# Experts' weights in pieces of 1 MB, the embedding's projection beside the router, and three input projections split

## The chip, the cores and the metric

The kernel runs on one core of a Trainium2 chip. The metric is the device time of one execution in microseconds. TensorE (PE) multiplies, VectorE (DVE), ScalarE (ACT) and GpSimd (POOL) work on SBUF and PSUM, and SyncE (SP) issues most of the DMAs.

## What is computed

256 tokens of width 1024, all in fp32, go through two blocks. The first has a mixer of a state-space part and attention, then a mixture of experts, then an embedding that is gated in. The second has RWKV7 beside a convolution, and then a feed-forward part. The end of the first block, where most of the change lies:

```python
h = rms_norm(x, moe_norm_w)
x = x + hier_moe(h, ...)   # 4 groups of 8 experts, width 256; best 2 of the best group
gate = jax.nn.sigmoid(rms_norm(x, ple_norm_w) @ w_ple_gate)
x = x + gate * (p @ w_ple)                # p: 256 x 256, an input of its own
```

In the second block three matrices of 1024 x 1024 (w_rkv) give r, k and v; small low-rank products give the decays and the rates; from these the scan of RWKV7 is computed.

## The kernel before

**A product.** Weights come as pieces of 128 x 1024 (0.5 MB) into the pool `raw` (four buffers). In the split way ACT makes the upper part `whi` (L238), DVE the rest `wlo` (L239), and PE multiplies whi by xh, whi by xl and wlo by xh (L275 for results with features on the partitions, L293 with tokens there). A unit of 512 output features has 32 products of 256 columns, so 96 rows of L275. In the plain way (tokens with an f in `PROG`) PE takes raw and fp32 input as they are (L266); each product is two rows of the trace, so 64 rows a unit, and ACT and DVE have no split to make.

**The order.** `PROG1` and `PROG` list units and steps. A scheduler then merges them, so that the instructions of an engine are interleaved, and every engine works through its own list in order. SP's list of DMAs is one too: one that waits for a free buffer holds those behind it. The second half's tokens are K0, K1, K2 (first half of r, k, v), R0, R1, R2 (their second half), L (low-rank products), A0 (`wkv_prep`: from k, r and L the factors AR and BK, on ACT, DVE and POOL), and B0 (L1269: products of AR and BK; G, L1271; then a DMA and the scan).

**The experts.** All 32 are computed: 8 steps q with 4 experts of 32 slots each, 24 pieces a step, 192 in all (100.7 MB). The first 38 pieces (`NFIRST`) are loaded ahead, during the mixer, into a ring of 40 buffers that are made of pools otherwise used for the mixer. P12 and P6 in `PROG1` and `expert_early` say where they are issued. Once the router has chosen (L805, L809 to L830 on DVE, L858), Pm is built, L966 gathers the tokens, L997 multiplies gate and up, L1018 down, and L1026 adds into four accumulators in PSUM (acc). They start as the residual: L949 multiplies X1 by the identity. After q = 0's gate and up all engines take a branch (L871 to L877): the `overflow` path serves experts with more than 32 tokens. In the profile it isn't taken.

**The embedding.** `ple` follows: L1034 copies acc to X, L376 transposes, L386 and L387 make xh and xl, and `ple_proj` computes U = p @ w_ple in the split way (L1056, 24 rows) before the gate's products (L293, 96 rows).

Of the kernel before, what the change touches and what calls it, by code (L numbers as in the profile page):

```python
# [100 lines left out]
def pack(i):  # L101
# [18 lines left out]
    d["w_gu"] = np.ascontiguousarray(wgu.reshape(8, 2, 2, 8, 128, 512).transpose(0, 3, 1, 4, 2, 5))  # L120
    d["w_dn"] = np.ascontiguousarray(i["w_exp_down"][0].reshape(8, 2, 2, 2, 128, 2, 512).transpose(0, 3, 5, 1, 4, 2, 6))
# [46 lines left out]
class Net:  # L168
# [535 lines left out]
    def mix1(self):  # L704
# [32 lines left out]
        self.expert_early(4)  # L737
        for c in range(2):
            self.transpose_chunk(M, c, mh, ml)
        self.expert_early(2)  # L740
        X1 = self.cst.tile([128, 2, 1024], F32, name="X1", tag="xp")
        self.ss1 = self.c1.tile([128, 2, 2], F32, name="ss1")
        self.hT = [self.mw.tile([128, 4, 256], F32, name=f"hT{c}", tag="mw") for c in range(2)]
# [54 lines left out]
    def route(self, hT, r):  # L798
# [68 lines left out]
    def overflow(self, acc, comb, rank, cnti):  # L867
# [4 lines left out]
        with tc.If(cv > 32):  # L872
# [6 lines left out]
            hT = self.hT  # L879
            gu, pt = [self.bank(tag="B") for _ in range(2)], self.bank((128, 256), "B")  # L880
            with tc.For_i(0, 8) as q:
                for e in range(4):
                    for kt in range(8):
                        w = self.t2(s="wf")
                        nc.gpsimd.dma_start(w, a["w_gu"][bass.ds(q, 1), kt, e // 2, :, e % 2, :].rearrange("o p n -> (o p) n"))
                        for tt in range(2):
                            PE.matmul(gu[tt], hT[kt // 4][:, kt % 4, tt * 128:tt * 128 + 128], w, start=(kt == 0), stop=(kt == 7))
                    wd = [[self.t2(s="wf") for _ in range(2)] for _ in range(2)]
                    for kt in range(2):
                        for h in range(2):  # L890
                            nc.gpsimd.dma_start(wd[kt][h], a["w_dn"][bass.ds(q, 1), kt, h, e // 2, :, e % 2, :].rearrange(
# [17 lines left out]
    def expert_fetch(self):  # L909

        a, n = self.a, self.wi
        q, k = divmod(n, 24)
        src = a["w_gu"][q, k // 2, k % 2] if k < 16 else a["w_dn"][q, (k - 16) // 4, (k - 16) // 2 % 2, k % 2]
        pool, tag = self.ring[n % len(self.ring)]
        if tag != "a8":
            w = pool().tile([128, 2, 512], F32, name=self.name("we"), tag=tag)
        elif self.half is None:
            self.half = self.a8(shape=(128, 4, 512), s="we")
            w = self.half[:, 0:2]
        else:  # L920
            w, self.half = self.half[:, 2:4], None
        self.nc.sync.dma_start(w, src)
        self.wi += 1
        self.early.append(w)
# [10 lines left out]
    def moe(self):  # L935
# [3 lines left out]
        self.expert_early(NFIRST - self.wi)  # L939
# [5 lines left out]

        acc = [[self.bank(tag="A", s="acc") for _ in range(2)] for _ in range(2)]
        for h in range(2):
            for tt in range(2):
                PE.matmul(acc[tt][h], self.ident, X1[:, tt, 512 * h:512 * h + 512], start=True, stop=False,  # L949
                          skip_group_check=True)  # L950
# [37 lines left out]
        nxt = gather(0)  # L988
        for q in range(8):
# [4 lines left out]
            for kt in range(8):  # L994
                w = [self.expert_piece() for i in range(2)]
                for e in range(4):
                    PE.matmul(gu[32 * e:32 * e + 32, :], xg[:, kt, 32 * e:32 * e + 32], w[e // 2][:, e % 2, :],  # L997
                              start=(kt == 0), stop=(kt == 7), skip_group_check=True)
            if q == 0:
                self.overflow(acc, comb, rank, cnti)  # L1000
# [13 lines left out]
            for kt in range(2):  # L1014
                for h in range(2):
                    w = [self.expert_piece() for i in range(2)]
                    for e in range(4):
                        PE.matmul(py[h][32 * e:32 * e + 32, :], gT[:, kt * 128 + 32 * e:kt * 128 + 32 * e + 32],  # L1018
                                  w[e // 2][:, e % 2, :], start=(kt == 0), stop=(kt == 1), skip_group_check=True)
            for h in range(2):  # L1020
# [8 lines left out]
        self.p = self.t2((128, 2, 256), s="p")  # L1029
        nc.sync.dma_start(self.p, a["pT"])  # L1030
# [9 lines left out]
    def ple_proj(self):  # L1040
# [3 lines left out]
        self.U = U = self.a8(shape=(128, 2, 1024), s="U")  # L1044
        ph, pl = (self.t2((128, 2, 256), F32R, s="ps") for _ in range(2))
        S.activation(ph, self.p, AF.Copy)
        V.tensor_sub(pl, self.p, ph.bitcast(F32))
        for c in range(2):
            hi, lo = self.split(self.fetch(a["w_ple"][c]))
            for tt in range(2):  # L1050
                ts = slice(128 * tt, 128 * tt + 128)
                ps = self.bank(tag="B")
                n = 0
                for kt in range(2):
                    for x, ww in ((ph, hi), (pl, hi), (ph, lo)):
# [689 lines left out]
```

## Time and profile before

| | us |
|---|---|
| three runs | 1242.92, 1243.56, 1244.0; median 1243.56 |
| the profiled execution | 1243.91 |
| its span, first to last instruction | 1242.2 |
| outside the span | 1.7 |
| PE busy in the span | 1146.0 (92%) |
| DVE, ACT, POOL busy | 693.8, 461.4, 109.7 |
| experts' gate, up and down, from L997's first to L1018's last row | 360.1 to 567.6 |
| mean granted clock of PE | 0.976 of full speed |

The times that are compared are those of the runs. The profile shows one execution. Its rows give starts from the span's beginning; a busy time can overlap with the next row, since matmuls are pipelined, so the distance of starts is the better measure of a group of equal rows.

### The profile page before, as it was taken

The numbers are of one execution on the slowest core, as the hardware profiler recorded it, in microseconds if no ns is written. First come the engines' busy times: TensorE is split into PE (matmuls) and PEld (weight loads), VectorE is DVE, ScalarE is ACT, GpSimd is POOL, SyncE is SP. The second block draws the span as 40 slices with busy tenths as digits, with TensorE's granted clock in tenths as the row PEclk, the third lists the DMA queues.
The fourth block names the chain that finished last, engine by engine and source line by source line (L and its number), as shares of the span: only waits on it lengthen the run. The fifth ranks groups of instructions, "written<-read, shape, count | busy, mean of one in ns | idle before, by whom it ended". The sixth has DMA issues, their size and how long they took to land.

```text
span 1242.2 us, 19656 instructions
## 1 busy us (share of the span) xinstructions
PE 1146.0 (92%) x7795; PEld 873.9 (70%) x7795; DVE 693.8 (56%) x1459; ACT 461.4 (37%) x835; POOL 109.7 (9%) x126
## 2 busy tenths in 40 slices
PE   5999999999979988877799899999999999999996
PEld 5898986667745433314697686778777788999995
DVE  4777677556532211104766527884988526656555
ACT  4644644444312000004654314332332215545453
POOL 0002321001100000000020402301200100000000
PEclk9999999999989999998899898899999999999999
DMA  8743555336769999994455244124422335555553
GB/s 301 279 157 115 153 170 180 109 118 245 276 255 409 409 409 409 409 409 168 134 182 204 93 139 125 52 70 111 111 70 69 102 125 191 177 187 186 190 186 116
DMA packets 82976, 242.20 MB, mean 195 GB/s; under 512 B 24160, under 2 KB 24416, under 8 KB 82496
## 3 DMA queue, kind: packets, MB, share of 16 engines
q1 hardware_dynamic: 80224, 231.11, 52.7%
q0 software_dynamic: 2224, 8.90, 2.5%
q8 instruction: 63, 1.03, 0.3%
q10 hardware_dynamic: 432, 0.89, 0.2%
q14 instruction: 33, 0.27, 0.1%
HBM read 234.31 MB, written 4.46 MB: 192 GB/s over the span
## 4 chain that ended last, share of the span: by engine, by line
PE 51%; DMA 8%; DVE 6%; ACT 2%; issue 1%; POOL 1%; DVEq 0%; ACTq 0%; SPq 0%; POOLq 0%
PE ps L266 12%; PE ps L275 9%; PE acc L293 7%; DMA we<-in_w_gu 5%; PE ps L1613 4%; PE ps L293 3%; PE ps L997 3%; DMA we<-in_w_dn 2%; PE ps L966 2%; PE ps L1018 2%; PE ps L1315 1%; DVE cv L1465 1%; PE acc L1026 1%; ACT whi L238 1%; PE ps L1056 1%
## 5 line engine op out<-in xcount | busy, mean ns | idle before, releaser
L239 DVE TENSOR_TENSOR wlo<-raw,whi 128x1024 fp32r<-128x1024 f32 (+1 forms) x178 | 225.7, 1272 | 149.9 <-ACT whi L238 144.8
L238 ACT ACTIVATE whi<-raw 128x1024 fp32r<-128x1024 f32 (+1 forms) x178 | 187.6, 1055 | 221.3 <-PE ps L275 78.6
L266 PE MATMUL ps<-x,raw 128*128 128x256 f32 x704 | 179.8, 402 | 5.3 <-issue 5.3
L266 PEld LDWEIGHTS ps<-x,raw 128*128 128x128 f32 x704 | 132.3, 196 | 30.9 <-issue 10.6
L275 PE MATMUL ps<-xh,whi 128*128 128x256 f32 x408 | 116.7, 287 | 4.4 <-ACT cv L446 1.5
L275 PE MATMUL ps<-xl,whi 128*128 128x256 f32 x408 | 115.1, 283 | 0.0
L275 PE MATMUL ps<-xh,wlo 128*128 128x256 f32 x408 | 114.2, 285 | 0.9 <-DVE wlo L239 0.8
L1465 DVE SCALAR_TENSOR_TENSOR cv<-up,par,cv 128x256 f32<-128x256 f32 x232 | 107.6, 500 | 2.6
L275 PEld LDWEIGHTS ps<-xh,whi 128*128 128x128 f32 x408 | 78.0, 191 | 6.8 <-ACT whi L238 3.4
L997 PE MATMUL ps<-we,xg 128*32 128x512 f32 x512 | 76.2, 597 | 4.3 <-DMA we<-in_w_gu 4.3
L275 PEld LDWEIGHTS ps<-xh,wlo 128*128 128x128 f32 x408 | 77.1, 191 | 2.1 <-DVE wlo L239 1.7
L275 PEld LDWEIGHTS ps<-xl,whi 128*128 128x128 f32 x408 | 78.1, 191 | 0.0
L275 PE MATMUL ps<-h,whi 128*128 128x256 f32 x256 | 72.1, 282 | 0.3 <-DVE l L387 0.3
L275 PE MATMUL ps<-h,wlo 128*128 128x256 f32 x256 | 71.7, 282 | 0.1
L275 PE MATMUL ps<-l,whi 128*128 128x256 f32 x256 | 71.7, 281 | 0.0
L293 PE MATMUL ps<-wlo,xh 128*128 128x512 f32 x128 | 50.7, 398 | 1.7 <-DVE wlo L239 1.7
L293 PE MATMUL ps<-whi,xh 128*128 128x512 f32 x128 | 50.9, 398 | 0.0
L293 PE MATMUL ps<-whi,xl 128*128 128x512 f32 x128 | 50.5, 394 | 0.0
L293 PE MATMUL acc<-wlo,fh 128*128 128x512 f32 x128 | 49.9, 390 | 0.0
L293 PE MATMUL acc<-whi,fl 128*128 128x512 f32 x128 | 49.9, 390 | 0.0
L293 PE MATMUL acc<-whi,fh 128*128 128x512 f32 x128 | 49.8, 389 | 0.0
L1018 PE MATMUL ps<-we,gT 128*32 128x512 f32 x256 | 44.1, 600 | 6.2 <-DVE gT L1012 3.5
(473 smaller groups left out, 2010.1 us busy)
## 6 DMA issues: line engine op xcount, KB each, us to landing
we<-in_w_gu SPq DMA_DIRECT2D x128, 512.0 KB, 10.2
we<-in_w_dn SPq DMA_DIRECT2D x64, 512.0 KB, 10.2
raw<-in_w_ff SPq DMA_DIRECT2D x64, 512.0 KB, 3.3
raw<-in_w_g SPq DMA_DIRECT2D x32, 512.0 KB, 3.3
raw<-in_w_qkv SPq DMA_DIRECT2D x24, 512.0 KB, 3.3
raw<-in_w_rkv SPq DMA_DIRECT2D x24, 512.0 KB, 3.3
raw<-in_w_o SPq DMA_DIRECT2D x16, 512.0 KB, 4.8
raw<-in_w_glu SPq DMA_DIRECT2D x16, 512.0 KB, 3.3
```

The costliest lines, as they stand in the source:

```text
L238: nc.scalar.activation(hi, r, AF.Copy)
L239: nc.vector.tensor_sub(lo, r, hi.bitcast(F32))
L266: pin(nc.tensor.matmul(out[f], r[:, k, f * 128:f * 128 + 128], xh[:, kt, :], start=(kt == 0), stop=(kt == 7)))
L275: pin(nc.tensor.matmul(out[f], w[:, k, c], x[:, kt, :], start=(kt == 0 and j == 0), stop=(kt == 7 and j == 2)))
L293: pin(nc.tensor.matmul(out[tt], x[:, x0 + k, s], w[:, k, :], start=(kt == 0 and j == 0), stop=(kt == last and j == 2)))
L966: PE.matmul(ps[:, f, :], X1[:, tt, ft * 128:ft * 128 + 128], Pm[:, tt, :], start=(tt == 0), stop=(tt == 1))
L997: PE.matmul(gu[32 * e:32 * e + 32, :], xg[:, kt, 32 * e:32 * e + 32], w[e // 2][:, e % 2, :], start=(kt == 0), stop=(kt == 7), skip_group_ ...
L1018: PE.matmul(py[h][32 * e:32 * e + 32, :], gT[:, kt * 128 + 32 * e:kt * 128 + 32 * e + 32], w[e // 2][:, e % 2, :], start=(kt == 0), stop=( ...
L1026: PE.matmul(acc[tt][h], PT[:, tt * 128:tt * 128 + 128], y, start=False, stop=(q == 7 and n == 1), skip_group_check=True)
L1056: PE.matmul(ps, x[:, kt, ts], ww[:, kt, :], start=(n == 0), stop=(n == 5))
L1465: pin(nc.vector.scalar_tensor_tensor(last, x[:, j:j + 256], self.P("cw", 8 * j + ft), o, op0=ALU.mult, op1=ALU.add))
L1613: pin(nc.tensor.matmul(out[f], r[:, k, 128 * f:128 * f + 128], z[:, kt, :], start=(kt == 0), stop=(kt == 7)))
```

## The change

Five things are edited at once.

1. Experts' pieces have 1 MB and 8 KB a partition: one piece holds a k tile of all four experts. There are 12 a step and 96 in all. The ring has 19 places; 14 take a piece as one DMA with 8 KB rows, and 5 are pairs of older buffers and take it as two DMAs with 4 KB rows. `NFIRST` is 19, the same 19.9 MB; the last of them is issued behind the first gather. `hT` is one tile, whose place is given up after the router, and `overflow` transposes X1 again.
2. p and w_ple are loaded at the end of the mixer (`ple_load`) into two of the buffers `raw`, and `ple_proj` stands right behind the router's products, in the plain way (now L1059), with U in a pool of its own. Loads and splits of it after the experts are gone.
3. The four products that start acc (L949, now L1004) come later: one before the first gather, three after q = 0's gate and up, ahead of the branch.
4. The down products go through h outside and kt inside, and y and its products for one h follow its two pieces.
5. In `PROG` K0, K2, L, K1 becomes K2, K1, K0, L, and R0, R1, R2 go from the plain way to the split way. Three pairs of later tokens change places. (`W0f` and `W1f` name the path that W0 and W1 took before; the new branch under W isn't used.)

```diff
-        q, k = divmod(n, 24)
-        src = a["w_gu"][q, k // 2, k % 2] if k < 16 else a["w_dn"][q, (k - 16) // 4, (k - 16) // 2 % 2, k % 2]
...
+        q, k = divmod(n, 12)
+        src = a["w_gu"][q, k] if k < 8 else a["w_dn"][q, (k - 8) // 2, k % 2]
+        pool, tags = self.ring[n % len(self.ring)]
+        shape = (128, 4 // len(tags), 512)
+        ws = [self.a8(shape=shape, s="we") if t == "a8" else pool().tile(list(shape), F32, name=self.name("we"), tag=t)
+              for t in tags]
+        for i, w in enumerate(ws):
+            self.nc.sync.dma_start(w, src[:, i * shape[1]:(i + 1) * shape[1], :])
...
+    def ple_load(self):
+
+        nc, a = self.nc, self.a
+        self.pp = self.act.tile([128, 1024], F32, name="pp", tag="P", bufs=2)[:, 0:512].rearrange("p (k t) -> p k t", k=2)
+        nc.sync.dma_start(self.pp, a["pT"])
+        self.wp = [self.fetch(a["w_ple"][c]) for c in range(2)]
...
+        self.ple_proj(0)
+        self.ple_proj(1)
         L = self.c1.tile([128, 2, 36], F32, name="L")
...
         nxt = gather(0)
+        self.expert_early(1)
...
             if q == 0:
+
+                for h in range(2):
+                    for tt in range(2):
+                        PE.matmul(acc[tt][h], self.ident, X1[:, tt, 512 * h:512 * h + 512], start=True, stop=False,
+                                  skip_group_check=True)
                 self.overflow(acc, comb, rank, cnti)
...
-            for kt in range(2):
-                for h in range(2):
-                    w = [self.expert_piece() for i in range(2)]
+            for h in range(2):
+                for kt in range(2):
+                    w = self.expert_piece()
...
-            hi, lo = self.split(self.fetch(a["w_ple"][c]))
...
-                for kt in range(2):
-                    for x, ww in ((ph, hi), (pl, hi), (ph, lo)):
-                        PE.matmul(ps, x[:, kt, ts], ww[:, kt, :], start=(n == 0), stop=(n == 5))
+            for kt in range(2):
+                PE.matmul(ps, self.pp[:, kt, ts], self.wp[c][:, kt, :], start=(kt == 0), stop=(kt == 1))
+            S.activation(U[:, tt, 512 * c:512 * c + 512], ps, AF.Copy)
...
-PROG = "K0 K2 L K1 A0 R0f R1f R2f B0 A1 U0f M0 C0 M0 M0 C1 G1f M0 M0 B1 O0 C2 U1f M1 C3! G0f M1 C6 M1 G3f M1 M1 C4! G2f C5 C7! O1 W0 S W1 D0 D1"
+PROG = "K2 K1 K0 L A0 R0 R1 R2 B0 A1 U0f M0 C0 M0 M0 C1 G1f M0 M0 B1 C2 O0 U1f M1 C3! C6 M1 G0f M1 G3f M1 M1 G2f C4! C5 C7! O1 W0f S W1f D0 D1"
-NEARLY = 12
-NFIRST = 38
+NEARLY = 5
+NFIRST = 19
...
-            n.ring = [(mw, "mw")] * NEARLY + [(None, "a8")] * 16 + [(raw, "raw")] * 4
-            n.ring += [(wsp, "whi"), (wsp, "wlo")] * 3 + [(mw, "mw")] * 2
+            n.ring = [(mw, ("mw",))] * NEARLY + [(None, ("a8",))] * 8 + [(wsp, ("whi", "wlo"))] * 3
+            n.ring += [(mw, ("mw",))] + [(raw, ("raw", "raw"))] * 2
```

**PE behind the router.** Before, PE's list had these rows between the router's last products (hT) and the first gather (X, Pm):

```order
L949 MATMUL acc_3318<-X_2984,const_82 128x512
L805 MATMUL ps_3227<-wr,hT_2987 128x36 [waits DVE_49]
L805 MATMUL ps_3227<-wr,hT_2986 128x36 x4
L805 MATMUL ps_3227<-wr,hT_2987 128x36 x4
L949 MATMUL acc_3320<-X_2984,const_82 128x512
L858 LDWEIGHTS ltb [waits DVE_49]
L858 MATMUL ps_3303<-sel,ltb 128x32 [waits PE_49]
```

In the changed kernel the same place reads:

```order
L806 MATMUL ps_3212<-wr,hT 128x36 x8
L1059 MATMUL ps_3233<-raw_3171,pp 128x512
L1059 MATMUL ps_3237<-raw_3173,pp 128x512 [waits DMAHW7_49,PE_49]
L1059 MATMUL ps_3237<-raw_3173,pp 128x512
L1059 MATMUL ps_3241<-raw_3173,pp 128x512 [waits Activation_49]
L1059 MATMUL ps_3241<-raw_3173,pp 128x512
L861 LDWEIGHTS ltb
L861 MATMUL ps_3304<-sel,ltb 128x32 [waits DVE_49]
```

The last product for acc has gone, and five of U's eight products (raw, pp) stand between the router and L861, which was L858; the other three have taken the places of L949 among the router's products.

**PE at the experts' end.** The last sums into acc (acc<-y), the transposes of X, and the embedding's products (ps are the split p) in the kernel before:

```order
L1026 MATMUL acc_3318<-y_4769,PT_4659 128x512 [waits DVE_49]
L1026 MATMUL acc_3320<-y_4769,PT_4659 128x512
L376 MATMUL ps_4822<-const_82,X_2984 128x128
L376 MATMUL ps_4831<-const_82,X_2984 128x128 [waits DVE_49]
L376 MATMUL ps_4840<-const_82,X_2984 128x128 [waits PE_49]
L376 MATMUL ps_4831<-const_82,X_2984 128x128 [waits DVE_49]
L376 MATMUL ps_4831<-const_82,X_2984 128x128 x2
L376 MATMUL ps_4840<-const_82,X_2984 128x128 x3
L1056 MATMUL ps_4875<-whi_4871,ps_4865 128x512 [waits DVE_49,PE_49,Activation_49]
L1056 MATMUL ps_4875<-whi_4871,ps_4866 128x512 [waits DVE_49]
```

In the changed kernel the last piece's down products (we_4813) and what follows:

```order
L1024 MATMUL ps_4782<-we_4813,gT_4779 32x512 [waits DMAHW5_49]
L1024 MATMUL ps_4782<-we_4813,gT_4779 32x512 x3
L1031 MATMUL acc_3319<-y_4819,PT_4716 128x512 [waits Activation_49]
L1031 MATMUL acc_3321<-y_4819,PT_4716 128x512
L1031 MATMUL acc_3319<-y_4820,PT_4716 128x512 [waits DVE_49]
L1031 MATMUL acc_3321<-y_4820,PT_4716 128x512
L293 MATMUL ps_4917<-whi_4921,xh_4860 128x512 [waits Activation_49]
L293 MATMUL ps_4918<-whi_4921,xh_4860 128x512
```

L1056's 24 rows are gone from here, and the gate's first products (L293) stand directly behind the last sums, ahead of half of the transposes.

**PE at R0.** Where B0's first products (AR, BK) stood before, between R0's last and R1's first products:

```order
L266 MATMUL ps_5903<-x_4807,raw_5934 128x256 x2
L1269 MATMUL ps_6061<-AR_5761,BK_5762 128x128 [waits Activation_49,Pool_49]
L1269 MATMUL ps_6062<-AR_5761,BK_5762 128x128 [waits DVE_49,Activation_49,Pool_49]
L1269 MATMUL ps_6061<-AR_5761,BK_5762 128x128 [waits Pool_49]
L266 MATMUL ps_5954<-x_4807,raw_5958 128x256 [waits DMAHW5_49,DVE_49,Activation_49]
L266 MATMUL ps_5954<-x_4807,raw_5958 128x256
```

In the changed kernel B0's products for two of four column groups stand ahead of the last 16 rows of R0:

```order
L275 MATMUL ps_5903<-xl_4855,whi_5997 128x256
L275 MATMUL ps_5904<-xh_4854,whi_5997 128x256
L275 MATMUL ps_5904<-xl_4855,whi_5997 128x256
L1270 MATMUL ps_6302<-AR_5762,BK_5763 128x128 [waits Pool_49]
L1270 MATMUL ps_6303<-AR_5762,BK_5763 128x128 [waits DVE_49,Pool_49]
L1270 MATMUL ps_6314<-AR_5762,BK_5763 128x128
L1270 MATMUL ps_6315<-AR_5762,BK_5763 128x128
```

Four more such rows of B0 follow, and only then R0's last 16. So those rows of R0, and R1 and R2 behind them, now wait for the second half of A0, which POOL finishes. Before, only three rows of B0 stood ahead of R1, and 29 came behind R2; now 14 come behind R2.

## Rows read from the trace of the kernel before

**Rows 1.** The page: traffic of the DMA engines in 40 slices of the span.
```profile
GB/s 301 279 157 115 153 170 180 109 118 245 276 255 409 409 409 409 409 409 168 134 182 204 93 139 125 52 70 111 111 70 69 102 125 191 177 187 186 190 186 116
```

**Rows 2.** Windows: busy time by engine (instructions), granted clock, DMA share, GB/s.
```profile
350.00:360.00 10.00, 6.43 (x37) 6.32 (x37) 5.97 (x35) 0.42 (x2) 0.00 (x0) 0.66 0.17 68
...
370.00:560.00 190.00, 165.56 (x1032) 66.99 (x1032) 32.30 (x88) 17.80 (x32) 0.84 (x2) 0.98 1.03 409
650.00:652.00 2.00, 1.96 (x17) 1.94 (x16) 1.22 (x5) 0.67 (x1) 0.00 (x0) 1.00 0.41 130
654.00:658.00 4.00, 3.54 (x27) 3.14 (x27) 2.30 (x6) 2.12 (x2) 0.00 (x0) 1.00 0.71 228
1000.00:1020.00 20.00, 20.00 (x94) 17.51 (x93) 5.39 (x14) 2.72 (x5) 0.00 (x0) 1.00 0.41 138
```

**Rows 3.** PE's timeline around the choice of experts: start, us, [idle before <-releaser].
```profile
348.15 1.10 PE L949 MATMUL acc<-X,const 128*128 128x512 f32 x2
352.84 0.21 PE L858 MATMUL ps<-sel,ltb 128*128 128x32 bf16 x1 [3.58 <-DVE sel L830]
...
353.89 6.26 PE L966 MATMUL ps<-Pm,X 128*128 128x128 f32 x32 [0.73 <-DVE Pm L957]
360.08 7.07 PE L997 MATMUL ps<-we,xg 128*32 128x512 f32 x64
371.31 1.04 PE L976 MATMUL ps<-comb,Pm 128*128 128x33 f32 x4 [4.15 <-PEq L872]
...
379.14 3.21 PE L1018 MATMUL ps<-we,gT 128*32 128x512 f32 x28 [0.90 <-DVE gT L1012]
```

**Rows 4.** The chain of waits around the experts' end: start, us, what.
```profile
566.60 1.01 PE ps L1018 x4
567.63 0.61 ACT y L1022
...
569.62 0.70 DVE X L1034
...
575.83 8.14 PE ps L1056 x24
583.97 21.34 PE ps L293 x94
```

**Rows 5.** The same chain in the second half's inputs.
```profile
657.55 13.69 PE ps L275 x112
...
682.85 0.72 PE ps L1246 x4
...
701.18 30.85 PE ps L266 x128
...
733.05 1.21 DVE G L1271 x2
...
735.49 1.16 PE ps L1269 x14
736.65 19.19 PE ps L266 x88
```

**Rows 6.** POOL's timeline at the end of A0.
```profile
701.56 0.73 POOL L1208 TENSOR_TENSOR BK<-rkv,cu 64x256 f32<-64x256 f32 x1
```

**Rows 7.** SP's queue from 345 to 362 us.
```profile
361.18 0.81 SPq L922 DMA_DIRECT2D we<-in_w_gu  x2
```

**Rows 8.** SP's queue of DMAs from 318 to 330 us.
```profile
318.32 4.02 SPq L230 DMA_DIRECT2D raw<-in_w_o  x3
```

**Rows 9.** SP's queue from 548 to 575 us.
```profile
547.81 6.73 SPq L922 DMA_DIRECT2D we<-in_w_dn  x6
...
562.31 0.33 SPq L230 DMA_DIRECT2D raw<-in_w_pg  x1
```

**Rows 10.** DMAs issued from 552 to 556 us: count, size, us to landing.
```profile
we<-in_w_dn SPq DMA_DIRECT2D x2, 512.0 KB, 10.2
```

**Rows 11.** The page's groups: count, busy us, mean ns, idle before.
```profile
L239 DVE TENSOR_TENSOR wlo<-raw,whi 128x1024 fp32r<-128x1024 f32 (+1 forms) x178 | 225.7, 1272 | 149.9 <-ACT whi L238 144.8
```

More of the change, by code (lines that the diff above doesn't have):

```diff
@@ L736, in mix1 @@
         mh, ml = self.a8(F32R, s="mh"), self.a8(F32R, s="ml")
[L737 removed]
+        self.expert_early(2)
         for c in range(2):
             self.transpose_chunk(M, c, mh, ml)
[L740 removed]
+        self.expert_early(1)
         X1 = self.cst.tile([128, 2, 1024], F32, name="X1", tag="xp")
         self.ss1 = self.c1.tile([128, 2, 2], F32, name="ss1")
[L743 removed]
+        self.hT = self.mw.tile([128, 2, 4, 256], F32, name="hT", tag="mw")
         self.wr = self.c1.tile([128, 8, 36], F32, name="wr")
@@ L878, in overflow @@
             V.memset(wo[1], 0.0)
-            hT = self.hT
-            gu, pt = [self.bank(tag="B") for _ in range(2)], self.bank((128, 256), "B")
+            X1 = self.X1
+            gu, pt = [self.bank(tag="B") for _ in range(2)], self.bank(tag="B")
+            pt, ht = pt[:, 0:256], pt[:, 256:512]
             with tc.For_i(0, 8) as q:
@@ L911, in expert_fetch @@
         a, n = self.a, self.wi
-        q, k = divmod(n, 24)
-        src = a["w_gu"][q, k // 2, k % 2] if k < 16 else a["w_dn"][q, (k - 16) // 4, (k - 16) // 2 % 2, k % 2]
[L914 to L922, printed above, removed]
+        q, k = divmod(n, 12)
[6 more added lines that the diff above has]
+            self.nc.sync.dma_start(w, src[:, i * shape[1]:(i + 1) * shape[1], :])
         self.wi += 1
-        self.early.append(w)
+        self.early.append([ws[e // shape[1]][:, e % shape[1], :] for e in range(4)])
     def expert_early(self, *n):
@@ L1013, in moe @@
             py = [self.bank(tag="B") for _ in range(2)]
-            for kt in range(2):
-                for h in range(2):
-                    w = [self.expert_piece() for i in range(2)]
+            for h in range(2):
+                for kt in range(2):
+                    w = self.expert_piece()
                     for e in range(4):
-                        PE.matmul(py[h][32 * e:32 * e + 32, :], gT[:, kt * 128 + 32 * e:kt * 128 + 32 * e + 32],
-                                  w[e // 2][:, e % 2, :], start=(kt == 0), stop=(kt == 1), skip_group_check=True)
-            for h in range(2):
+                        PE.matmul(py[h][32 * e:32 * e + 32, :], gT[:, kt * 128 + 32 * e:kt * 128 + 32 * e + 32], w[e],
+                                  start=(kt == 0), stop=(kt == 1), skip_group_check=True)
                 yh, yl = (self.t2(dt=F32R, s="y") for _ in range(2))
@@ L1557, in branches @@
             elif op == "W":
-                self.gated(gates[n], y, a["w_rwp"][n], pin)
+                if "f" in tok:
+                    self.gated(gates[n], y, a["w_rwp"][n], pin)
+                else:
+                    if not ys:
+                        ys = [self.keep.tile([128, 8, 256], F32R, name="y" + m, tag=f"x{m}2") for m in "hl"]
+                        self.split_act(y, *ys, V)
+                    for f, ps in enumerate(self.feat(*ys, a["w_rwp"][n], pin=pin)):
+                        V.tensor_mul(gates[n][:, f, :], ps, gates[n][:, f, :])
             elif op == "D":
```

59 lines of the change are left out of this document (27 added, 32 removed).

## The prediction

> **What bounds the kernel now.** I read the page's slices of traffic first: six slices in a row stand at 409 GB/s, which no other slice reaches [rows 1]. The windows show the same place: from 370 to 560 us the DMA engines' share is 1.03 (all 16 busy) at 409 GB/s, while PE has 165.56 us of work in 190 [rows 2]. So the experts' stage is bound by their weights, and it lasts from the first load after the ring was full to the last landing. Outside of it PE is the bound, except where it waits for a chain on other engines. Three such places are touched: the choice of experts, the embedding, and A0. The timeline of PE shows the first: 3.58 us of idle time ahead of L858, then a gather of 6.2 us in a window with a clock of 0.66 [rows 2, 3]. The chain of waits shows the second: from the last down products (566.60) it passes y, the copies of X and a split to L1056, and reaches L293 at 583.97 [rows 4]. It shows the third too: K1 ends at 671.24, R1 starts at 701.18 [rows 5], and POOL writes the last factor BK until 702.29 [rows 6].
>
> **First load after the router.** SP issues nothing for the ring until 361.18 [rows 7], because L997, which frees the first place, starts at 360.08 [rows 3]. Five of U's products now follow the router. L949 shows the price of a product of this form: two rows in 1.10 us [rows 3]; five of them overlap and take some 4.7, 5.5 at the most. So they fill 348.2 to 352.9, and L861 could not start before 352.8 anyway: they cost next to nothing there, and cover the idle time. One of the acc products falls into the 0.73 us ahead of L966. PE then enters the gather without the gap. The distance from L966 to L997 is 6.19 us at 0.66; at full clock it is 6.19 x 0.66 = 4.1. The first load comes 2.1 us earlier (bounds 0, if the clock stays low, and 3).
>
> Three acc products (2.8 us) now stand ahead of the branch, which costs PE 4.15 us in any case [rows 3]. So L1018 comes at 379.14 - 2.1 + 2.8 = 379.8. By then 16 half pieces, freed by q = 0's gate and up, have been loaded: 8.39 MB at 409 GB/s is 20.5 us from 359.1, so until about 380 and a latency. A place freed at 380.6 gives traffic again some 2 us later. I take a hole of 1.5 us (bounds 0 and 3). Both together: -0.6 us (bounds -3 and +3).
>
> L1059 also needs p and w_ple. They follow the last three loads of w_o, which SP has issued by 322.34 [rows 8], and are wanted 20 us later, so I take no wait.
>
> **Rows of 8 KB.** After the ring was full 100.66 - 19.92 = 80.74 MB are left, 197.4 us at 409 GB/s. No saturated stretch of before has longer rows. What doubling a row gives is bounded by the traffic per share: 130 / 0.41 = 317 GB/s where the low-rank weights with 2 KB rows are loaded, 228 / 0.71 = 321 and 138 / 0.41 = 337 with 4 KB rows [rows 2]. That is 1.3 to 6.3% for 2 to 4 KB. If each packet has a fixed part, the next doubling gives half as much, and 14 of 19 pieces have it: 0.5 to 2.4%, 0.9 to 4.6 us. Below, nothing: six slices at the same 409 may be a ceiling that no row length moves. I take -3 us, the middle of the two rows' results, with 0 and -4.6 as bounds.
> [...]
>
> **The embedding.** The last half piece is issued at 554.21 (six issues from 547.81, 6.73 us, less 0.33 for the last) [rows 9] and lands 10.2 us later [rows 10], at 564.4. Its products start only at 566.60, since sums of h = 0 and transposes stand ahead of them. With h outside these are done before the last piece, whose products can start as it lands. It has eight rows rather than four, so 0.8 us more at about 0.2 a row (28 rows from 379.14, 3.21 us, bound it by 0.11 [rows 3]). They end at 566.2 instead of 567.6: -1.4 us.
>
> Before, 16.4 us lie between 567.6 and L293 at 583.97: y, sums, X, then xh, the split of p and w_ple, and L1056 with 8.14 us [rows 4]. What remains is y (0.6) and its rest on DVE (as long), one split of w_pg that stands in between there (1.3 [rows 11]), two copies of X (1.4) and two parts of xl, each shorter than a copy: 5.5 us, so -10.9. w_pg was issued at 562.31 [rows 9], behind w_ple; now its buffers are freed by the pieces before the last. The steps just named are the least; if the splits of w_pg come late, 8.5.
> One thing is given back. L1056's 24 rows take 8.14 us, against 24 x 21.34 / 94 = 5.4 at L293's pace: PE comes out of idle time at the lower clock, and L293 will now pay that: +2.7. Sum for the embedding: -1.4 - 10.9 + 2.7 = -9.6 us (bounds -6 and -12.3).
>
> **Inputs of the second half.** K0, K1, K2 and L are the same 384 products in another order (112 rows take 13.69, 0.122 each [rows 5]). L is last now, and K0's copies from PSUM stand beside its splits on DVE: +1.5 (bounds 0 and 4). A0 then runs from L's end. Before it took 671.24 to 702.29, 31.05 us; inv_root, which needs only k, held L1246 until 682.85 [rows 5], and now lies beside L. Against it two splits of R0 on DVE and four on ACT come into the chain. I take 28 us (25 to 34).
>
> Behind the last BK there remain: 16 rows of R0 (2.0), B0's products in between (0.5), R1 and R2 with 192 x 0.122 = 23.4, the lower clock after idling (30.85 for 128 plain rows against 128 x 19.19 / 88 = 27.9: +2.9), B0's last 14 rows (1.2) and most of the wait for G's copies that stands in the chain now (1.0 of 1.21): 31.0. The stage takes 1.5 + 28 + 31.0 = 60.5 us. Before it took 671.24 to 736.65, 65.4. So -4.9 us (bounds -11 and +5). A plain unit is 64 x 0.218 = 14.0 us, a split one 96 x 0.122 = 11.7, so R1 and R2 give 4.5 of this, and R0 lies beside A0 either way.
>
> What follows (U0f on) is plain and keeps its order but for three exchanged pairs; nothing in the rows prices them, and PE is at work there, so 0 (bounds -2 and +2).
>
> **Sum.** -0.6 - 3.0 - 9.6 - 4.9 = -18.1. The profiled execution has 1243.91 us, 0.35 above the median. So 1225.5 us in the scale of the runs.
>
> **Rivals.**
> (a) The 8 KB rows give nothing and the hole after the branch has its full 3 us: 1225.5 + 3.0 + 1.5 = 1230. For it speak the equal slices [rows 1]. The change of size would then only make fewer DMAs.
> (b) A0 is the bound. The scheduler put eight rows of B0 ahead of R0's last 16, and PE can't pass a row that waits. If the splits of R0 on ACT and DVE hold up A0's own steps (six splits, at DVE's 1.27 us 7.6 in all [rows 11]), A0 takes 34 and L comes 4 late: the stage is 3.6 us longer than before, and 1225.5 + 4.9 + 3.6 = 1234. For it speaks the lone chain from 671 to 702; against it that POOL, which splits nothing, has the end of it.
> (c) More is won: A0 at 25 us, no hole, 4.6 for the rows: 1225.5 - 3 - 1.5 - 1.6 = 1219.
> (d) Slower than before: longer packets move more slowly. Then the stage that is bound by them pays. The other terms are -15.1, so it decides where 197.4 us becomes 197.4 + 15.1 + 2.5 = 215, at 375 GB/s; at 365 the stage takes 221.2, and the sum is 1243.6 - 15.1 + 23.8 = 1252. Against it: per share, 4 KB rows are faster than 2 KB ones [rows 2].
>
> **Chances.** Forecast as summed 0.54, (a) 0.14, (b) 0.17, (c) 0.09, (d) 0.06. About 0.2%, 2.5 us, is what can be told from no change. Cases between (b) and before, with the embedding's term at its bound of -6 too, give the chance of no change. From these: faster 0.88, same 0.05, slower 0.07. The range goes from 1214, below (c), to 1238, above (b).
>
> **What will show it.** Right: SP's first load after the ring at about 359; a share of 1.0 with 410 to 421 GB/s from 385 to 555; L293 about 7 us after the last landing; R1 in 96 rows. Wrong: a share under 0.9 around 380; PE waiting at L1270 longer than 12 us; traffic under 409; or a row of L1059 that waits for a DMA.

## The result, and the profile after

The changed kernel takes 1222.8 us (median of four runs, 1219.9 to 1224.9) against 1243.3 for the kernel before on the same chip: a ratio of 0.983, with a 95% interval of 0.981 to 0.985. The profiled execution has a span of 1221.3 us, 20.9 less than before's. The mean granted clock is 0.972 (0.976 before).

The page's traffic in 40 slices, which answers to [rows 1]:

```profile
GB/s 310 245 156 106 171 140 189 129 112 204 291 355 399 420 415 420 416 416 227 138 187 104 122 226 75 54 54 156 70 71 87 105 119 190 189 187 188 193 184 112
```

Windows (columns as in [rows 2]): the two stretches shown before, and the place where the hole was forecast.

```profile
350.00:360.00 10.00, 9.85 (x79) 5.72 (x81) 5.66 (x31) 2.62 (x5) 0.00 (x0) 1.00 0.82 307
...
370.00:560.00 190.00, 158.91 (x1041) 61.11 (x1040) 33.36 (x85) 17.80 (x35) 0.85 (x2) 0.96 1.01 412
375.00:380.00 5.00, 4.47 (x19) 1.03 (x19) 0.66 (x3) 0.60 (x1) 0.00 (x0) 0.66 1.01 392
380.00:385.00 5.00, 5.00 (x26) 1.61 (x26) 1.30 (x4) 0.98 (x2) 0.00 (x0) 1.00 0.98 360
400.00:540.00 140.00, 116.53 (x790) 45.41 (x788) 23.88 (x64) 11.83 (x23) 0.00 (x0) 0.96 1.02 418
```

The stage is still bound by its weights (share 1.02), and the equal 409 of before was no ceiling: 418 GB/s stand in 400 to 540. The hole is a dip, not a hole: (418 - 392 + 418 - 360) x 5 / 418 = 1.0 us.

PE's timeline around the choice of experts, which answers to [rows 3]:

```profile
346.98 4.54 PE L1059 MATMUL ps<-raw,pp 128*128 128x512 f32 x10
351.66 0.18 PE L861 MATMUL ps<-sel,ltb 128*128 128x32 bf16 x1
...
352.73 3.75 PE L966 MATMUL ps<-Pm,X 128*128 128x128 f32 x32
356.41 7.07 PE L998 MATMUL ps<-we,xg 128*32 128x512 f32 x64
363.41 2.84 PE L1004 MATMUL acc<-X,const 128*128 128x512 f32 x6
367.68 0.60 PE L976 MATMUL ps<-comb,Pm 128*128 128x33 f32 x4 [1.43 <-PEq L875]
...
375.53 3.52 PE L1024 MATMUL ps<-we,gT 128*32 128x512 f32 x13 [0.90 <-DVE gT L1018]
```

No idle time is left between the router and L998, the clock in the window is 1.00 instead of 0.66, and the gather takes 3.68 us rather than 6.19. Look at L1004: three products (2.84 us) stand ahead of the branch, and the wait for PE's sequencer behind them is 1.43 us where it was 4.15. The branch ran beside them.

SP's queue (as [rows 7, 9]) and the landing of the last pieces (as [rows 10]):

```profile
357.54 0.33 SPq L927 DMA_DIRECT2D we<-in_w_gu  x1
...
539.25 5.44 SPq L927 DMA_DIRECT2D we<-in_w_dn  x5
```

```profile
we<-in_w_dn SPq DMA_DIRECT2D x1, 1024.0 KB, 13.8
```

The last piece is issued at 544.36 (539.25 + 5.44 - 0.33), and is there at 558.2; before it was 564.4. At the experts' end PE's timeline (in place of [rows 4]) has no gap above 1.1 us any more:

```profile
558.28 1.07 PE L1024 MATMUL ps<-we,gT 128*32 128x512 f32 x8
560.13 1.47 PE L1031 MATMUL acc<-y,PT 128*128 128x512 f32 x4 [0.78 <-ACT y L1027]
562.66 0.74 PE L293 MATMUL ps<-whi,xh 128*128 128x512 f32 x2 [1.06 <-ACT xh L386]
```

The chain of waits from there on, which answers to [rows 4 to 6]:

```profile
565.55 20.30 PE ps L293 x88
...
595.49 6.43 PE ps L378 x32
601.92 22.54 PE ps L275 x186
...
628.05 4.15 DMA raw<-in_w_l
...
634.01 2.74 DMA raw<-in_w_l
...
678.43 1.63 POOL BK L1208
680.14 1.61 POOL BK L1209
681.79 1.22 PE ps L1270 x6
683.01 3.57 PE ps L275 x16
...
687.22 23.45 PE ps L275 x192
710.68 1.98 PE ps L1270 x28
712.65 7.12 PE ps L266 x32
```

L293 ends at 585.86, 19.45 us earlier than the 605.31 of [rows 4]. From L378 to the end of B0 the stage takes 116.9 us (121.4 before): 4.5 more are won. Then 3.2 are lost again: from the end of B0 to the first product of the scan (out of T0T) pass 45.0 us, and 41.8 before. In between PE idles at A1, and what follows runs at half clock:

```profile
744.18 1.14 PE L1247 MATMUL ps<-iv,const 32*128 32x256 f32 x4 [2.52 <-DVE iv L304]
```

```profile
741.00:744.00 3.00, 0.67 (x4) 0.24 (x2) 2.90 (x4) 1.15 (x2) 2.30 (x3) 1.00 1.05 298
744.00:747.00 3.00, 2.82 (x12) 1.78 (x12) 1.75 (x6) 0.45 (x1) 0.00 (x0) 0.55 0.16 63
747.00:757.00 10.00, 10.00 (x23) 5.87 (x20) 7.48 (x17) 6.14 (x12) 4.85 (x5) 0.50 0.00 0
757.00:760.00 3.00, 3.00 (x26) 2.37 (x25) 2.51 (x5) 2.22 (x5) 2.98 (x3) 0.84 0.51 160
```

From there to the end it is 463.9 us in both kernels, so no effect of the three exchanged pairs of tokens shows in the sum.

### The profile page after: what moved, and what is told of

The parts are those of the page before. It is cut to its first block, busy times and chain, and to the rows that moved or that the text cites. A ratio compares the mean times of both kernels' runs of the same rounds, so it can differ in the third digit from the quotient of the medians.

```text
span 1221.3 us, 19771 instructions
## 1 busy us (share of the span) xinstructions
PE 1128.9 (92%) x7883; PEld 865.2 (71%) x7883; DVE 704.9 (58%) x1468; ACT 471.0 (39%) x844; POOL 115.8 (9%) x126
## 4 chain that ended last, share of the span: by engine, by line
PE 41%; DVE 7%; DMA 2%; ACT 2%; POOL 1%; issue 1%; DVEq 0%; SPq 0%; ACTq 0%; POOLq 0%
PE ps L275 11%; PE ps L266 8%; PE acc L293 7%; PE ps L1621 4%; PE ps L293 3%; PE ps L1316 1%; DVE cv L1466 1%; DMA raw<-in_w_l 1%; PE ps L1270 1%; DVE wlo L239 1%; ACT whi L238 1%; PE ps L1351 1%; PE ps L1367 1%; PE ps L378 1%; DMA raw<-in_w_o 0%
## 5 line engine op out<-in xcount | busy, mean ns | idle before, releaser
L239 DVE TENSOR_TENSOR wlo<-raw,whi 128x1024 fp32r<-128x1024 f32 (+1 forms) x188 | 239.4, 1278 | 151.3 <-ACT whi L238 145.8
L275 PE MATMUL ps<-xh,whi 128*128 128x256 f32 x504 | 145.7, 290 | 3.2 <-ACT cv L446 1.5
L275 PE MATMUL ps<-xh,wlo 128*128 128x256 f32 x504 | 142.7, 289 | 1.4 <-DVE wlo L239 1.3
L275 PE MATMUL ps<-xl,whi 128*128 128x256 f32 x504 | 143.4, 285 | 0.0
L266 PE MATMUL ps<-x,raw 128*128 128x256 f32 x512 | 133.9, 404 | 0.0
L266 PEld LDWEIGHTS ps<-x,raw 128*128 128x128 f32 x512 | 94.4, 195 | 18.8 <-issue 4.4
L275 PEld LDWEIGHTS ps<-xh,whi 128*128 128x128 f32 x504 | 97.7, 194 | 7.0 <-issue 2.1
L275 PEld LDWEIGHTS ps<-xh,wlo 128*128 128x128 f32 x504 | 96.4, 194 | 3.3 <-DVE wlo L239 2.3
L275 PEld LDWEIGHTS ps<-xl,whi 128*128 128x128 f32 x504 | 97.7, 194 | 0.0
L998 PE MATMUL ps<-we,xg 128*32 128x512 f32 x512 | 70.3, 617 | 8.7 <-DMA we<-in_w_gu 8.7
L293 PE MATMUL ps<-wlo,xh 128*128 128x512 f32 x128 | 50.9, 399 | 1.6 <-DVE wlo L239 1.6
L293 PE MATMUL ps<-whi,xh 128*128 128x512 f32 x128 | 50.7, 399 | 1.3 <-ACT xh L386 1.3
L293 PE MATMUL ps<-whi,xl 128*128 128x512 f32 x128 | 50.6, 395 | 0.0
L998 PEld LDWEIGHTS ps<-we,xg 128*32 128x32 f32 x512 | 15.3, 111 | 48.9 <-issue 24.1
L293 PE MATMUL acc<-wlo,fh 128*128 128x512 f32 x128 | 49.9, 390 | 0.0
L293 PE MATMUL acc<-whi,fl 128*128 128x512 f32 x128 | 49.9, 390 | 0.0
L293 PE MATMUL acc<-whi,fh 128*128 128x512 f32 x128 | 49.8, 389 | 0.0
```

Of the source, the lines that this page charges most:

```text
L239: nc.vector.tensor_sub(lo, r, hi.bitcast(F32))
L266: pin(nc.tensor.matmul(out[f], r[:, k, f * 128:f * 128 + 128], xh[:, kt, :], start=(kt == 0), stop=(kt == 7)))
L275: pin(nc.tensor.matmul(out[f], w[:, k, c], x[:, kt, :], start=(kt == 0 and j == 0), stop=(kt == 7 and j == 2)))
L293: pin(nc.tensor.matmul(out[tt], x[:, x0 + k, s], w[:, k, :], start=(kt == 0 and j == 0), stop=(kt == last and j == 2)))
```

## The experiments

In all of them the changed kernel is the base. "Stage" is the distance from the start of L378's first product to that of B0's last. "Tail of A1" is the distance from there to the first product with T0T. Each kernel was profiled once. In the six kernels whose edits lie outside the stage (the changed one and experiments 1, 2, 3, 4 and 7) it takes 114.0 to 117.3 us, so a stage that differs by 3 us or less doesn't show an edit's effect by itself.

**1 and 2. Rows of 4 KB and of 2 KB.** The DMAs keep 1 MB each; the weights are laid out so that a partition's part is cut in two or four.

```diff
-            self.nc.sync.dma_start(w, src[:, i * shape[1]:(i + 1) * shape[1], :])
+            g = 2 // len(ws)          # 4 // len(ws) for rows of 2 KB
+            self.nc.sync.dma_start(w.rearrange("p (g e) n -> p g e n", g=g),
+                                   src[i * g:(i + 1) * g].rearrange("g p e n -> p g e n"))
```

> Pieces stay 1 MB and one DMA each, but every row is cut in two of 4 KB (the weights lie in memory as two halves). Theory (each packet has a fixed part, about 9 ns by 409 GB/s before and 418 after): 409 GB/s from 400 to 540 us, the last landing 4 us later, 1226 to 1228 us. Rival (fewer and larger DMAs gave the traffic): still 418 GB/s and 1222 to 1224 us.

> As before, with rows of 2 KB: 1 MB in one DMA, four rows a partition. Theory (9 ns a packet): 85 ns for 2 KB, so 386 GB/s, the stage 15 us longer than with 8 KB, about 1238 us. Rival (a ceiling from 2 or 4 KB upward): 409 GB/s, as with 4 KB.

The window from 400 to 540 us, first with 4 KB:

```profile
400.00:540.00 140.00, 114.72 (x772) 44.98 (x772) 23.69 (x64) 11.25 (x22) 0.00 (x0) 0.95 1.03 409
```

and with 2 KB:

```profile
400.00:540.00 140.00, 114.84 (x740) 43.74 (x742) 22.19 (x59) 10.26 (x20) 0.00 (x0) 0.90 1.05 387
```

So the row's length sets the traffic here, and the size of a DMA does not: 387, 409, and 418 for the mixture, and rows of 4 KB give 409 with 0.5 MB a DMA (the kernel before) and with 1 MB. From the first two, one of 16 engines takes 84.7 ns for 2 KB and 160.2 for 4 KB; with a fixed part for each row that is, as an estimate, 75.6 for 2 KB of bytes and 9.1 besides. By that estimate 8 KB alone would give 421, and the mixture 418, as measured. In time: 1236.1 us with 2 KB (ratio 0.994, 0.992 to 0.996) against 1222.8. With 4 KB L293 starts at 566.37, 3.7 us later than in the changed kernel (1.0 of it from a later first load), and yet the time is the same, 1223.9 (0.984, 0.979 to 0.988): A1's tail has 40.1 us instead of 45.0. The part on the rest, at the end, comes back to that.

**3. U behind the experts**, still plain and with its loads there.

```diff
-        self.ple_load()              # at the mixer's end
-        self.ple_proj(0)             # behind the router's products
-        self.ple_proj(1)
...
+        self.ple_load()              # in ple, ahead of the gate's products
+        self.ple_proj(0)
+        self.ple_proj(1)
```

> The embedding's load and its products, still in the plain way, stand behind the experts again; nothing else is changed. Theory (the move gave most of the 13 us between last landing and the end of L293, and covers the choice of experts): PE idles 3 us before L861, the gather takes about 6 us again, the first load comes 2.5 us later, and the end of L293 comes 6 to 10 us later after the last landing: 1231 to 1236 us. Rival (the order of the down products and of the splits gave it, and plain products without splits fill idle time): 1224 to 1228 us, with the end of L293 under 4 us later after the last landing.

It takes 1227.7 us (0.987, 0.984 to 0.991). PE's timeline shows both halves of the edit:

```profile
352.25 0.19 PE L858 MATMUL ps<-sel,ltb 128*128 128x32 bf16 x1 [3.58 <-DVE sel L830]
...
353.28 6.67 PE L963 MATMUL ps<-Pm,X 128*128 128x128 f32 x32 [0.73 <-DVE Pm L954]
```

```profile
566.75 7.13 PE L1056 MATMUL ps<-raw,pp 128*128 128x512 f32 x16 [0.94 <-DVE xl L387]
573.32 0.80 PE L293 MATMUL ps<-whi,xh 128*128 128x512 f32 x1
```

The idle 3.58 us and the slow gather are back, and the granted clock from 350 to 360 us is 0.66 as it was before, so it is the products behind the router that keep the clock up there; the first gate and up product (L998) starts 3.5 us later. With U gone the scheduler also put all four products for acc ahead of the router's last ones. At the end L293 is done 9.4 us later. Of these 2.9 come back in the stage (114.0) and 1.4 in A1's tail, without a cause that the trace shows. The time is 4.9 us longer, less than I expected; since the intervals overlap a little, what U's place is worth is shown at these two places of the trace and hardly in the total.

**4. The four products for acc at the front again**, before the first gather.

> All four products that start the accumulators stand ahead of the first gather. Theory (the branch runs beside PE's queue, so three of them cost nothing ahead of it): the first load comes 2.8 us later, L976 too, and the distance from L998's last row to L976 stays at 4.2 us; 1224 to 1226 us. Rival (the branch begins when PE has finished, and they cost 2.8 us there): the distance falls to 1.4 us, L976 stays at 367.7 and the time at 1222 to 1224 us.

```profile
370.05 1.04 PE L980 MATMUL ps<-comb,Pm 128*128 128x33 f32 x4 [4.13 <-PEq L875]
```

The theory's distances came out. With nothing between the last L1002 (L998 in the changed kernel) and the branch, the whole 4.1 us are idle time; with three products there, 1.4. The branch's end is tied to the instruction ahead of those products, and they are free. Ahead of the gather they are not: gate and up start 2.4 us later (358.84), and so does L980. Yet the time is 1222.7 us (0.984, 0.981 to 0.987), the same, and not the 1224 to 1226 of the theory: the stage is 2.1 us shorter (114.8), within its spread.

**5. R0, R1 and R2 plain**, in the new order of K and L.

```diff
-PROG = "K2 K1 K0 L A0 R0 R1 R2 B0 ...
+PROG = "K2 K1 K0 L A0 R0f R1f R2f B0 ...
```

> K2, K1, K0, L stay, and R0, R1, R2 go back to the plain way. In PE's list no product of B0 then stands ahead of R1 or R2. Theory (A0 is the bound, R1 and R2 follow it in either way, and plain units cost 2.3 us more each): from the first transpose of the second half (L378) to B0's last product 2 to 5 us longer than 116.9, 1224 to 1228 us. Rival (B0's products ahead of R0's last rows hold PE up; without them R1 and R2 run beside A0): this stage 4 us shorter or more, under 1219 us.

My theory fell. It is faster, not slower: 1214.5 us (0.974, 0.973 to 0.976), and the stage has 114.1 instead of 116.9. PE's timeline, and POOL's last BK:

```profile
662.09 9.76 PE L266 MATMUL ps<-x,raw 128*128 128x256 f32 x44
674.77 29.58 PE L266 MATMUL ps<-x,raw 128*128 128x256 f32 x128 [2.92 <-DVE rkv L1147]
704.28 4.89 PE L1270 MATMUL ps<-AR,BK 64*128 64x128 f32 x64
```

```profile
675.20 0.73 POOL L1209 TENSOR_TENSOR BK<-rkv,cu 64x256 f32<-64x256 f32 x1
```

R0 has no splits to wait for, so all of it lies beside A0, and R1 starts at 674.77, not at 687.22. A0 itself is shorter too: from L's last product (651.23) to the last BK it takes 24.7 us, where it took 29.7 in the changed kernel with splits beside it. POOL's last two BK steps take 0.72 and 0.73 us here; there they take 1.63 and 1.60, while DVE works at two splits (678.28 to 681.15). Why POOL is slower in that stretch isn't shown. R1 and R2 then take 6.1 us more, and B0's products, all of them behind R2 now, 2.9 more. That leaves 3. Of the 5.6 us between the profiled executions 2.8 lie in the stage and 2.9 in A1's tail; the medians differ by 8.3, so how much of the gain is the stage's isn't shown.

**6. The old order of K and L, with R split.**

```diff
-PROG = "K2 K1 K0 L A0 R0 R1 R2 B0 ...
+PROG = "K0 K2 L K1 A0 R0 R1 R2 B0 ...
```

> R0, R1, R2 stay split, and the order is K0, K2, L, K1 again. Theory (A0 starts when k is there, and inv_root lies in its chain again): the stage is 2 to 4 us longer than 116.9, 1224 to 1227 us. Rival (L's waits for its loads cost more at the end of the four than in the middle): the stage is as long or shorter, 1219 to 1223 us.

The stage takes 120.5 us, 3.6 more than in the changed kernel; the time is 1222.1 (0.981, 0.979 to 0.982), where A1's tail gives 1.7 back. With experiment 5 that makes a table of the stage: old order and plain 121.4 (the kernel before, which lacks the other edits too), old order and split 120.5, new order and split 116.9, new order and plain 114.1. The order of K and L is worth 7.3 us with R plain and 3.6 with R split, both outside the spread; what the table has for the split (0.9 gained in the old order, 2.8 lost in the new one) lies within it.

**7. The memsets of W on GpSimd.** In A1 DVE's memset of W waits for a DMA that reads W (it takes 5.49 us in the chain, of which DVE idles 0.95), with iv, for which PE waits, queued behind it.

```diff
-        E.memset(W, 0.0)
-        E.memset(W.rearrange("p a b -> p (a b)")[:, 0:256:17], 1.0)
+        G.memset(W, 0.0)
+        G.memset(W.rearrange("p a b -> p (a b)")[:, 0:256:17], 1.0)
```

> The two memsets of W, which on DVE stand in the middle of A1's inv_root and wait there for a DMA, go to POOL. Theory (that wait delays PE's L1247, and PE's clock falls in it): from B0's last product to the first one on T0T 40 to 42 us instead of 45, 1219 to 1221 us. Rival (PE's own list of head sums sets it): 44 to 45 us and 1222 to 1224.

```profile
737.03 0.27 DVE L1281 MEMSET W<- 128x256 f32 x1 [0.95 <-DMA blkb<-W]
```

That is the wait in the changed kernel. With the memsets on GpSimd the time is 1218.3 us (0.979, 0.977 to 0.980), PE's idle time at L1247 falls from 2.52 to 1.48 us, and the tail is 39.65: it looks like the theory. That moving the memsets takes 1.0 us out of the idle time is shown; that it also shortened the half clock (13.7 to 3.4 us), which is most of the tail's gain, is not.

**8. v as late as it is used**: K2 behind A0.

```diff
-PROG = "K2 K1 K0 L A0 R0 R1 R2 B0 ...
+PROG = "K1 K0 L A0 K2 R0 R1 R2 B0 ...
```

> The order is K1, K0, L, A0, K2, R0, R1, R2: K2 gives v, which A0 doesn't read. Theory (A0's 28 to 30 us behind L are the bound, and PE has only 10 us of work in them): K2's 11.7 us move beside A0; the stage is 8 to 11 us shorter than 116.9, 1212 to 1215 us. Rival (K2's splits and copies on ACT and DVE lengthen A0 by as much as they take, 8 us): the stage is 0 to 4 us shorter, 1219 to 1223 us.

1217.0 us (0.977, 0.975 to 0.978), but the stage is only 1.5 us shorter (115.4). A0 is done 15 us earlier (its last BK at 666.75), and all three units of R now follow it: TensorE's list has B0's first rows ahead of K2's last 16, as it had them ahead of R0's. A1's tail has 39.1 us there, and 4.8 of that gain are given back behind T0T (468.7 us to the end, against 463.9).

**9 to 12. B0 held behind R2, and combinations.** If one early row of B0 blocks PE, taking it out of the way should free 15 us.

```diff
-                    PE.matmul(ps[h][:, q, :], BK[H(h), q, c, :, :], AR[H(h), q, c, :, :], start=True, stop=True)
+                    self.pin(hf == 0 and c == q == h == 0)(
+                        PE.matmul(ps[h][:, q, :], BK[H(h), q, c, :, :], AR[H(h), q, c, :, :], start=True, stop=True))
```

> The changed kernel with one edit: the first of B0's 32 products is held in program order, so that none of them stands ahead of R0's last rows any more; R0, R1 and R2 stay split and all else stays. Theory (one product placed early blocks the engine: behind A0 lie R0's last 16 rows, R1 and R2, 30.9 us from L1270 at 681.79, only because TensorE can't pass L1270, which waits for BK): R0, R1 and R2 run beside A0, behind it only B0 is left, and the stage from L378 to the end of B0 is some 15 us shorter, 102 instead of 116.9, if the splits of R1 and R2 do not lengthen A0. Time 1208 (1204 to 1213). Rival 1 (the engines that split are the limit): the splits of R1 and R2 stand in DVE's and ACT's way beside A0's own steps, BK comes 8 to 15 us later, the stage is 112 to 117, time 1218 to 1223. Rival 2 (the clock): A0 without TensorE's gap leaves the clock up, and the loss of 3 us at A1 goes too; then 2 to 3 us less than the theory's.

> b0_pin with the two memsets of W on GpSimd. By the theory of b0_pin the stage is 102 and the rest 39.7 from the end of B0 to T0T: 1203 (1199 to 1208). By its rival 1 (splits hold up BK) 1213 to 1218. If A1 then starts without a gap anyway (rival 2), the memsets give nothing, and it equals b0_pin.

> The order K1 K0 L A0 K2 R0 R1 R2 (as v_last), R0 to R2 plain, the first of B0's products held behind them, and the memsets of W on GpSimd. Plain R units need 64 rows of 0.218 us each, 14.0 us, and no splits. Theory: with only K1, K0 and L ahead of it, A0 starts some 7.5 us earlier than in the changed kernel, at 644.6, and is done after 29.7, at 674; beside it lie K2 (7.5) and R0 to R2 (42); TensorE is then busy throughout and the stage is the sum of its work, 192 + 192 rows x 0.122 + 192 x 0.218 + waits for loads (some 5) + B0 (3.5) = 97 us; time 1197 (1193 to 1206). Rival (loads are the limit, since w_k, w_v, w_l, w_q and w_r follow each other through one ring whose places come free with the products): the stage is 105 to 112, time 1206 to 1214.

> The changed kernel with two edits that were measured one by one: R0, R1 and R2 plain (r_plain, 1214.5, stage 2.8 us shorter) and the two memsets of W on GpSimd instead of DVE (w_pool, 1218.3, 5.3 us less between the end of B0 and the first T0T product). Theory (they act at two places and the sums hold): the stage stays at 114.1, and from the end of B0 to T0T 39.6 to 40.1 instead of r_plain's 42.1, so 2.0 to 2.5 us under r_plain: 1212. Rival (what w_pool gains is the clock behind a short idle time, which r_plain has partly won already by its longer unbroken run of products): same as r_plain, 1214 to 1215.

| | time, us | ratio (95%) | stage | tail of A1 | half clock in it |
|---|---|---|---|---|---|
| B0 held | 1215.1 | 0.976 (0.973 to 0.978) | 113.2 | 38.75 | 3.4 |
| and memsets on GpSimd | 1219.6 | 0.979 (0.975 to 0.982) | 115.5 | 42.4 | 10.2 |
| K2 late, R plain, B0 held, memsets | 1221.5 | 0.980 (0.978 to 0.983) | 120.4 | 43.3 | 13.7 |
| R plain and memsets | 1213.0 | 0.975 (0.973 to 0.977) | 112.8 | 43.2 | 13.7 |

The last column is worked out from the granted clock of windows of 2 us.

Holding B0 wins 3.7 us of the stage (113.2, just outside the spread), none in the kernel with the memsets (115.5, as in experiment 7 without it), and not 15. PE's timeline with B0 held shows what came in its place:

```profile
670.43 0.58 PE L275 MATMUL ps<-xh,wlo 128*128 128x256 f32 x1 [4.30 <-DVE wlo L239]
...
678.67 0.39 PE L275 MATMUL ps<-xh,wlo 128*128 128x256 f32 x1 [2.75 <-DVE wlo L239]
...
705.52 4.88 PE L1271 MATMUL ps<-AR,BK 64*128 64x128 f32 x64
```

and DVE's timeline why:

```profile
676.64 0.84 DVE L1207 TENSOR_TENSOR rkv<-rkv,av 128x256 f32<-128x256 f32 x1
677.40 1.21 DVE L239 TENSOR_TENSOR wlo<-raw,whi 128x1024 fp32r<-128x1024 f32 x1
```

R0's last split stands behind A0's steps in DVE's list. In the changed kernel it stood there too (678.28), hidden behind the wait for BK. So rival 1 is right in kind, but not in size: the last BK is written at 679.27 to 680.9, no later than in the changed kernel, where splits stand beside A0 too. In both kernels the splits hold up A0, by the 5 us of experiment 5, and A0 holds up the splits. PE goes on at 678.67 instead of 682.94. With K2 behind A0 the same waits fall on K2, and R's plain units, which don't need DVE, stand behind it in PE's list: 672.64 to 715.25, and a stage of 120.4.

For the memsets the table gives no gain: with them the tail is 42.4 beside 38.75 without, and R plain has 43.2 with them and 42.1 without. It doesn't test the theory, though, since in these two kernels there is next to no wait to remove: DVE's memset waits 0.12 us with B0 held and not at all with R plain. What it does show is that the tail differs by 3.7 us where nothing but the memsets' engine changed. R plain with the memsets came out at 1213.0 where I had expected 1212, but not for the reason given: its tail is longer than expected, and it is the stage (112.8) and the rest behind T0T (460.4 instead of 464.6) that are shorter.

## Why the prediction was right, step by step

The forecast was 1225.5 and the measured time is 1222.8, in the range, and faster, as the chances had it. The sum was -18.1; the medians differ by 20.5 and the profiled spans by 20.9. That the sums come so close is luck in part: single terms miss by up to 3.6 us, and the largest two, the embedding and the rest, nearly cancel. By its terms, in the profiled executions:

| term | forecast | measured | |
|---|---|---|---|
| first load | -2.1 | -3.65 | gather at full clock -2.5, and the mixer ended 1.2 earlier |
| three acc products ahead of the branch | L1018 2.8 later, counted in the hole | 0 | |
| hole | +1.5 | +1.0 | a dip to 360 GB/s |
| rows of 8 KB | -3.0 | -4.2 | 80.74 MB at 418 instead of 409 |
| longer flight of the last piece | none | +0.6 | what is left of -6.2 at the landing |
| embedding | -9.6 | -13.2 | |
| second half's inputs | -4.9 | -4.5 | |
| the rest | 0 | +3.1 | A1 |

**First load.** Right in mechanism: PE stays busy behind the router, the clock stays at 1.00 and the gather runs at it (3.68 us instead of 6.19). The experiment with U behind the experts shows the reverse, idle time (3.58 us) and slow gather (6.60) together. The step that failed is "costs PE 4.15 us in any case": those 4.15 us run in the sequencer while products queued earlier are still at work, so products between were free here (2.84 us of them).

**Rows.** Right in mechanism and mis-sized: I took the middle of two rows' results because six slices at 409 looked like a ceiling. 409 was what rows of 4 KB give. My rule "the next doubling gives half as much" was the better guide: 387 to 409 is 5.7%, and 409 to the estimated 421 would be 2.9%; the mixture of 4 and 8 KB gave 2.2% (409 to 418). In the total this term can't be told from no change: with 4 KB the time is 1.1 us more, inside its interval, since A1 took another course.

**Embedding.** The steps hold: the last products end 1.15 us behind the landing (3.2 before), which makes -2.05 for the forecast's -1.4, and from there to L293's end it is 11.15 shorter (forecast 10.9 less the 2.7 given back). What failed is "L293 will now pay that: +2.7". The granted clock stays at 1.00 from 556 to 586, through idle times of 0.8 and 1.1 us, and L293's 88 rows keep the pace of before (0.231 us each, 0.227 in [rows 4]). The mechanism isn't refuted, though. In four kernels with the same idle times at the same place (2 KB rows, acc at the front, the old order of K and L, B0 held) half clock stands for 3.4 us at L293's start, and L293 takes 0.7 to 0.9 us longer from its first to its last row. Here is B0 held:

```profile
563.00:567.00 4.00, 3.79 (x14) 3.25 (x15) 3.86 (x8) 4.00 (x11) 0.00 (x0) 0.57 0.38 132
```

So the price was 0 to 0.9 us and not 2.7. No run takes back the order of the down products alone; what it gives is read from the landing in the trace.

**Second half's inputs.** The lengths of the parts were read rightly: A0 took 29.7 us (forecast 28), what stands behind it 30.9 (forecast 31.0), K and L 50.2 (52.3 by the forecast's +1.5). L doesn't run through, though: it waits for the loads of w_l (4.15 and 2.74 us in the chain). That the sum of -4.9 came out is luck all the same. The gain is in the order of K and L (7.3 us with R plain), and the split gives none: without it the stage isn't longer (114.1 against 116.9) and the time is 8.3 us less. The forecast priced R1 and R2 shorter by 4.5 and noted that R0 "lies beside A0 either way". That is the step that failed: split, its last 16 rows don't lie beside A0; plain, they do. Rival (b) had named both parts of the cause, the block by B0's rows and the splits that hold up A0 (5.0 us of the 7.6 that it put on them); taking the block away showed the next one behind it, DVE's list.

**The rest.** Zero was wrong by 3.1 us, more than the 2 allowed. In all kernels of this study PE idles in A1 for 1.5 to 2.9 us, and then runs at half clock (granted 0.50) for a time within the tail: not at all with K2 late alone, 3.4 us with B0 held, with the memsets alone and with 4 KB rows, 10.2 in the kernel before, 13.7 in the changed one. In the four with 3.4 us or less the tail takes 38.75 to 40.1 us, in the ten others 41.8 to 45.5. Here is K2 late alone, after an idle time of 2.22 us:

```profile
741.18 0.70 PE L1247 MATMUL ps<-iv,const 32*128 32x256 f32 x4 [2.22 <-DVE iv L304]
```

```profile
744.00:747.00 3.00, 3.00 (x12) 1.63 (x11) 2.93 (x8) 2.43 (x6) 0.73 (x1) 1.00 0.00 0
747.00:757.00 10.00, 7.90 (x60) 5.93 (x59) 10.00 (x18) 5.69 (x10) 8.28 (x10) 1.00 0.15 52
```

What decides the length stays open. It follows neither the idle time (2.20 us in the kernel with B0 held and 2.33 with the memsets besides, yet 3.4 and 10.2 us of half clock) nor an edit. Each kernel was profiled once, so these 5 us may fall differently in another execution of the same kernel. The runs' mean granted clocks speak for that: with R plain they are 0.973 in the profiled execution (1217.3 us) and 0.985 in the fastest (1211.8). The tail's differences are as large as several terms here, and I take no difference in total under 5 us as shown where the tails differ so.

**A better version.** With R plain the time is 1214.5, with the memsets besides 1213.0; their intervals (0.973 to 0.976 and 0.973 to 0.977) lie below that of the changed kernel (0.981 to 0.985), and the two can't be told apart. So the change without the split of R0 to R2 beats both kernels.

## What to carry to other kernels

Two edits to one stage need to be tried apart: here the better order hid that the split in the same stage had become a loss, because it put PE's rows behind splits on an engine that was not free (DVE), and made A0 itself 5 us longer (29.7 instead of 24.7). The equal slices of traffic were a ceiling only for the row length that made them (409 GB/s with 4 KB, 418 with 8 KB in 14 of 19 places); cut the rows in two to see where it is. When a block is taken out of an engine's list, look first at what the rows behind it wait for: with B0 held, 3.7 of the 15 us that I expected were won in one kernel, and none in the other.

## What the runs showed of the hardware

- A DMA row cost 9.1 ns besides its bytes on each of 16 busy engines, an estimate from 387 and 409 GB/s for 2 and 4 KB (the mixture's 418 GB/s fits it), and 0.5 and 1 MB a DMA gave the same 409 with rows of 4 KB.
- A branch's 4.1 us on PE's sequencer run beside products that are already queued: 4.13 us idle without, 1.43 with 2.84 us of products there.
- After nearly equal idle times of 2.19 to 2.33 us in A1 the clock stayed up, or stood at half for 3.4, 10.2 or 13.7 us; A1's tail took 39.1 us in the first case, 38.75 and 40.1 with 3.4, 42.4 with 10.2, and 43.2 and 43.3 with 13.7.
- After the same idle times of 0.8 and 1.1 us at the experts' end the clock stayed up in the changed kernel and fell for 3.4 us in four others.
